# Five small experts of a routed layer: from exact parts in float32r to plain float32 in column strips

## The chip, the core and the metric

The kernel runs on one core of a Trainium2 chip, the other cores idle. The metric is the device time of one execution in microseconds; the time before is the median of three runs. A core has a matrix engine (PE, and PEld for its weight loads), three more engines that compute (DVE, ACT, POOL), SP, which issues most transfers here, and 16 DMA engines between the chip's memory (HBM) and the core's own (SBUF). PE writes its products to PSUM, eight banks of 128 rows by 512 float32 columns.

## The reference, cut to what matters

A network of four layers on 256 tokens of 1024 features, in float32 throughout. The change touches only the last sublayer, a mixture of eight experts, two of them for each token:

```
def moe_swiglu(h, w_router, b_router, w_gate, w_up, w_down):
    logits = (h @ w_router).astype(F32) + b_router.astype(F32)
    top_logits, top_idx = lax.top_k(logits, TOP_K)       # TOP_K = 2 of 8
    ...
    # per expert e: (silu(h @ w_gate[e]) * (h @ w_up[e])) @ w_down[e], times the token's gate
```

Each expert has three matrices of 1024 x 3584 (down: 3584 x 1024). For the inputs of `setup_inputs()` the reference sends 146, 114, 95, 61, 35, 30, 24 and 7 tokens to the eight experts, in falling order: 512 places in all.

## The kernel before

The kernel runs the layers one after the other and streams every weight once, in units of 1 MB ([128, 2048] float32, names `raw`). For products PE takes operands in float32r, a form with fewer bits that a full-width product goes through once. To keep float32 accuracy, `w` (lines 215 to 234) splits each unit in two exact parts: ACT casts 1024 columns at a time to float32r (`hi`, line 229), DVE subtracts (`lo`, line 231). `mm3` (lines 242 to 246) then multiplies three times: hi by hi, lo by hi, hi by lo. A `raw` buffer is free again when its unit is split. In the expert layer there are six: four of the pool `wp` and two of the pool `moew` (lines 221 and 222).

`moe` (from line 1801) orders the experts by their counts: rank 0 has the most tokens. `CAPS` gives the slots of each rank. A one-hot matrix of tokens by slots gathers the slots' features (`gather`, `gather_slim`) and adds the results back to the tokens (`scatter`). An expert's hidden columns come in 7 steps of 512, each of six units: two of gate, two of up, two of down. There are three shapes of work:

- `Narrow` (ranks 1 to 3, 128 slots): slots are the stationary operand, weights move, 512 columns at a time, three products each (`mm3`).
- `Slim` (ranks 4 to 7, 64 slots): both parts of a slot's features are two rows of one product, so that hi and lo of the weights are enough (two products, line 1963); a product with `ii` adds the two rows again (line 1976).
- `wide` (rank 0, 256 slots): the weights are stationary, the slots move, 256 at a time, three products. It is a generator: 21 steps of two units, and two scatters. `turn` calls one step after every third turn of the Slim items, three turns an item (lines 2070 to 2077).

The main loop (lines 2079 to 2102) walks through the items of the ranks 4, 1, 5, 2, 6, 3, 7 and keeps one item ahead: gate of this item, `prep` of the last (transposes), up of this, down of the last. A scheduler places instructions within this order; SP issues the units in the order in which `w` was called, each when its buffer is free. Tokens beyond an expert's slots are handled by code behind a branch (line 2105) that these counts don't enter.

Of the kernel before, what the change touches and what calls it, by code (L numbers as in the profile page):

```python
# [56 lines left out]
def constants():  # L57
# [23 lines left out]
    c["c_ii"] = (t[:, None] % 64 == np.arange(64)[None]).astype(f)  # L81
# [100 lines left out]
# ---------------------------------------------------------------- the program  # L182
class Net:
# [31 lines left out]
    def w(self, src, n=2048):  # L215
        """a weight unit: its raw tile and, in pieces of 1024 columns, its two exact parts;
        the result gives the parts of a range of columns"""
# [3 lines left out]
        self.turn = (self.turn + 1) % 6 if self.more else 0  # L221
        pool, bufs = (self.wp, 4) if not self.more or 0 < self.turn < 5 else (self.more, 2)
# [37 lines left out]
    def rows(self, factors=False):  # L260
        """for products of rows not normed: self.eps, eps for the norms that follow; the factors of the rows' own norm"""
# [9 lines left out]
    def split(self, ps, hi, lo, scale=None):  # L271
        """hi and lo, the exact parts of ps (times the column scale)"""
# [7 lines left out]
    def rms(self, xs, eps=1e-6, pool=None):  # L280
        """x * rstd, token-major"""
# [10 lines left out]
    def norm_t(self, xs, gname, i, perm=False, out=None, xn=None):  # L292
        """feature-major parts of rms_norm(x) * g, its rows normed already; perm: token 8c + 2q + h at column 128h + 32q + c"""
# [23 lines left out]
    def proj_a(self, xt, src, kt=8, mt=2, halves=False):  # L317
        """one unit of columns: feature-major, [128, mt, 256]"""
# [41 lines left out]
    def proj_d(self, xt, src, order=None, end=False):  # L360
        """[256, 1024] = x @ w, token-major, four banks"""
# [80 lines left out]
    # ---- first block  # L442
# [10 lines left out]
    def t5_bias(self, ph):  # L453
        """bias[q, h, c] of the distance 128 + q - c, -1e30 below zero"""
# [52 lines left out]
            # columns: [s0 t0 | s0 t1 | s1 t1]  # L507
# [10 lines left out]
    def out_steps(self, o, src, n=4, done=None):  # L518
        """steps of o @ w, a unit at a time"""
# [81 lines left out]
        # k_idx | w_idx  # L601
# [14 lines left out]
        # norms of c_q and c_kv  # L616
# [21 lines left out]
        # indexer: k_idx feature-major twice over, q_idx feature-major  # L638
# [26 lines left out]
        # a key of the future gets -1e30 exactly, then the 64 largest of each row are marked  # L665
# [14 lines left out]
        # queries, keys and values  # L680
# [27 lines left out]
    def small_a(self, w, xt, n, put):  # L708
        """x of 256 features times w [256, n], feature-major; put(m, psum of two blocks, 2)"""
# [1673 lines left out]
```

## Time and profile before

| | us |
|---|---|
| median of 3 runs | 2505.92 (2504.39 to 2511.6) |
| the profiled execution, its span | 2511.8 |
| first unit of an expert issued at | 1446.49 |
| PE busy, whole span | 2381.2 (95%) |
| DVE busy, whole span | 1850.4 (74%) |
| ACT busy, whole span | 1503.8 (60%) |
| mean rate of the DMA over the span | 236 GB/s |

The span is the time from the first to the last instruction of the program in the profiled execution, the table's second row. A busy PE isn't a PE at its peak: the spacing of the starts in the timeline tells what one product takes, its duration also holds the latency. The expert layer, from 1446 to the end, has 336 units and reads 352.3 MB, three fifths of what the kernel reads in all.

### The profile page before, as it was taken

To read this page: it belongs to the slowest core of one execution; us is meant where nothing else is said; L and a number is where in the kernel's file an instruction comes from. 1 tells how busy PE (TensorE), PEld (TensorE's weight loads), DVE (VectorE), ACT (ScalarE), POOL (GpSimd) and SP (SyncE) were. 2 spreads that over 40 slices of the span, in tenths; PEclk is the share of its full clock that TensorE was granted. 3 is DMA by queue.
4 is the path that set the end of the run, shared out by engine and by line. 5 is a ranking of instruction groups with operands and counts; after the bars stand their busy time and mean duration, and the time that the engine had idled before them with its cause. 6 is when DMAs were issued, how large, how long until landed. Compare 5 with 4: busy or idle time off the path is not lost.

```text
span 2511.8 us, 37371 instructions
## 1 busy us (share of the span) xinstructions
PE 2381.2 (95%) x14223; PEld 2025.2 (81%) x14223; DVE 1850.4 (74%) x2606; ACT 1503.8 (60%) x2256; POOL 169.7 (7%) x153
## 2 busy tenths in 40 slices
PE   8999999989987999999989979999999999999997
PEld 7789888879876787999878868777888778877785
DVE  5566567896787275555667498888888888898888
ACT  5655456634453266444556477777676677676776
POOL 0000003033602000000121000000000000000000
PEclk9999999999998899999999989999999999999999
DMA  7436553555623453555424098889888988889886
GB/s 280 159 137 233 186 188 118 196 179 194 251 93 104 123 216 116 185 186 188 183 101 155 26 361 342 321 341 362 331 323 328 349 340 342 333 311 347 344 323 249
DMA packets 100472, 593.06 MB, mean 236 GB/s; under 512 B 12275, under 2 KB 25748, under 8 KB 32316
## 3 DMA queue, kind: packets, MB, share of 16 engines
q1 hardware_dynamic: 86816, 562.72, 59.9%
q10 hardware_dynamic: 11452, 17.38, 1.9%
q0 software_dynamic: 2016, 10.49, 1.2%
q8 instruction: 114, 1.87, 0.3%
q14 instruction: 74, 0.61, 0.1%
HBM read 571.41 MB, written 19.14 MB: 235 GB/s over the span
## 4 chain that ended last, share of the span: by engine, by line
PE 51%; DVE 6%; ACT 3%; issue 2%; POOL 1%; DMA 0%; ACTq 0%; DVEq 0%; POOLq 0%
PE acc L245 7%; PE acc L244 7%; PE acc L246 7%; PE pt L1963 6%; PE pt L245 6%; PE pt L244 6%; PE pt L246 6%; DVE lo L231 4%; PE acc L1990 3%; ACT hi L229 2%; PE pt L1976 1%; PE pt L920 1%; POOL rstd_r L257 1%; PE pt L1937 0%; DVE x L1896 0%
## 5 line engine op out<-in xcount | busy, mean ns | idle before, releaser
L231 DVE TENSOR_TENSOR lo<-raw,hi 128x1024 fp32r<-128x1024 f32 x1042 | 1251.4, 1242 | 311.9 <-ACT hi L229 310.8
L229 ACT CAST hi<-raw 128x1024 fp32r<-128x1024 f32 x1042 | 1046.9, 1051 | 465.5 <-PE pt L245 161.3
L244 PE MATMUL pt<-xh,hi 128*128 128x256 f32 (+1 forms) x1112 | 314.9, 283 | 2.6 <-DVE xl L278 2.0
L245 PE MATMUL pt<-xl,hi 128*128 128x256 f32 (+1 forms) x1112 | 312.5, 281 | 0.2 <-DVE xl L278 0.2
L246 PE MATMUL pt<-xh,lo 128*128 128x256 f32 (+1 forms) x1112 | 312.3, 281 | 0.0
L244 PEld LDWEIGHTS pt<-xh,hi 128*128 128x128 f32 (+1 forms) x1112 | 210.3, 189 | 8.3 <-issue 2.5
L245 PEld LDWEIGHTS pt<-xl,hi 128*128 128x128 f32 (+1 forms) x1112 | 210.0, 189 | 2.8 <-DVE xl L278 0.6
L246 PEld LDWEIGHTS pt<-xh,lo 128*128 128x128 f32 (+1 forms) x1112 | 210.2, 189 | 0.0
L244 PE MATMUL pt<-hi,xh 128*128 128x256 f32 x512 | 146.5, 286 | 1.4 <-DVE ol L278 1.4
L245 PE MATMUL pt<-lo,xh 128*128 128x256 f32 x512 | 144.4, 282 | 0.0
L246 PE MATMUL pt<-hi,xl 128*128 128x256 f32 x512 | 144.1, 282 | 0.0
L246 PE MATMUL acc<-hi,hlo 128*128 128x512 f32 x344 | 137.3, 400 | 6.3 <-DVE hlo L276 6.3
L244 PE MATMUL acc<-hi,hhi 128*128 128x512 f32 x344 | 137.7, 400 | 3.5 <-ACT hhi L275 3.5
L245 PE MATMUL acc<-lo,hhi 128*128 128x512 f32 x344 | 136.9, 398 | 0.0
L245 PE MATMUL pt<-lo,xgh 128*128 128x512 f32 x336 | 135.9, 405 | 1.0
L244 PE MATMUL pt<-hi,xgh 128*128 128x512 f32 x336 | 133.9, 399 | 2.1 <-DVE x L1896 2.1
L246 PE MATMUL pt<-hi,xgl 128*128 128x512 f32 x336 | 132.8, 395 | 0.0
L245 PE MATMUL acc<-x0l,hi 128*128 128x256 f32 x448 | 124.6, 279 | 0.0
L244 PE MATMUL acc<-x0h,hi 128*128 128x256 f32 x448 | 124.4, 279 | 0.0
L246 PE MATMUL acc<-x0h,lo 128*128 128x256 f32 x448 | 123.9, 280 | 0.0
L244 PEld LDWEIGHTS pt<-hi,xh 128*128 128x128 f32 x512 | 98.8, 193 | 3.3 <-DVE ol L278 2.2
L245 PEld LDWEIGHTS pt<-lo,xh 128*128 128x128 f32 x512 | 98.7, 193 | 0.9 <-DVE lo L231 0.3
(723 smaller groups left out, 4841.3 us busy)
## 6 DMA issues: line engine op xcount, KB each, us to landing
raw<-in_moe_gate SPq DMA_DIRECT2D x112, 1024.0 KB, 6.1
raw<-in_moe_up SPq DMA_DIRECT2D x112, 1024.0 KB, 6.5
raw<-in_moe_down SPq DMA_DIRECT2D x112, 1024.0 KB, 6.8
raw<-in_mlp_up SPq DMA_DIRECT2D x32, 1024.0 KB, 4.8
raw<-in_mlp_dn SPq DMA_DIRECT2D x32, 1024.0 KB, 4.8
raw<-in_ff_g SPq DMA_DIRECT2D x11, 1024.0 KB, 4.8
raw<-in_ff_u SPq DMA_DIRECT2D x11, 1024.0 KB, 4.8
raw<-in_ff_d SPq DMA_DIRECT2D x11, 1024.0 KB, 4.8
```

Of the source, the lines that this page charges most:

```text
L229: nc.scalar.copy(hi[:, :c], raw[:, o:o + c])
L231: nc.vector.tensor_tensor(lo[:, :c], raw[:, o:o + c], hi[:, :c].bitcast(F32), op=OP.subtract)
L244: mm(out, l[0], r[0], start=first, stop=False)
L245: mm(out, l[0], r[1], start=False, stop=False)
L246: mm(out, l[1], r[0], start=False, stop=last)
L257: nc.gpsimd.tensor_tensor(r, v, self.mhalf[:, :width], op=OP.pow)
L920: nc.tensor.matmul(po[:, d * 256:d * 256 + 256], v[:, m, d * 128:d * 128 + 128], PT[:, m * 256:m * 256 + 256], start=m == 0, stop=m == 1)
L1963: mm(p, l, q, start=u + k + i == 0, stop=u * 4 + k + i == 8)
L1976: mm(p[:, o:o + 64], me.z[i][:, j * 128:j * 128 + 128], ii, start=True, stop=True)
L1990: mm(me.acc[c], me.hT[:, 2 * u + j].rearrange("p a c -> p (a c)"), q, start=f + u + j + i == 0, stop=f == 6 and u + j + i == 3)
```

## The change

Ranks 3 to 7 get 64, 64, 32, 32 and 32 slots (before: rank 3 had 128 and the Narrow form, ranks 4 to 7 had 64 and the Slim form). Their weights are not split (`whole=True`): PE takes them from `raw` as plain float32, and the gathered features (`xc`) too, in one tile of 256 columns for all five. A product with 64 (32) slots fills 64 (32) of the array's 128 columns; two (four) such products, each with its own quarter or half of the hidden columns, are issued in turn and write their own rows of one PSUM bank (class `Few`, `strip`). `prep` transposes two (one) blocks, `down` does the same with the output columns in one PSUM bank, and `scatter_few` adds strip by strip. The one-hot rows for it are made again at each expert's sixth item (`few_rows`). The order of the ranks is 3, 1, 4, 2, 5, 6, 7, and a step of `wide` follows every fourth turn in ranks 3 and 4, every third in ranks 5 to 7.

```diff
-CAPS = (256, 128, 128, 128, 64, 64, 64, 64)
+MORE = 2
+CAPS = (256, 128, 128, 64, 64, 32, 32, 32)
...
-    def w(self, src, n=2048):
+    def w(self, src, n=2048, whole=False):
...
         nc.sync.dma_start(raw[:, :n], src)
+        if whole:
+            return lambda o, c: raw[:, o:o + c]
...
+            xg = ph.tile([128, 8, 256], F32, name="xc")
+            for k2 in range(4):
+                p = self.pt()
+                for j in range(2):
+                    for i, src in enumerate((hh, hl)):
                         for t in range(2):
+                            mm(p[:, j * 256:j * 256 + 256], src[:, t, (2 * k2 + j) * 128:(2 * k2 + j + 1) * 128], OH[:, t], start=i + t == 0, stop=i + t == 2)
+                (nc.scalar.copy if k2 % 2 else nc.vector.tensor_copy)(xg[:, 2 * k2:2 * k2 + 2], p.rearrange("p (j c) -> p j c", j=2))
...
+        def scatter_few(acc, OT, r, then=None):
+            n = CAPS[r]
+            G, w = 128 // n, 8 * n
+            y = ph.tile([128, 512], F32, name="yf", bufs=2)
+            nc.scalar.copy(y[:, 0:w], acc[0][:, 0:w])
+            for t in range(2):
+                ps = [self.pt() for _ in range(G)]
+                for g, p in enumerate(ps):
+                    mm(p[:, 0:w], OT[g * n:g * n + n, t * 128:t * 128 + 128], y[g * n:g * n + n, 0:w], start=True, stop=True)
+                for g, p in enumerate(ps):
+                    o = xs[t][:, g * w:g * w + w]
+                    stt(o, p[:, 0:w], gater[:, t, r:r + 1], o, op0=OP.mult, op1=OP.add)
...
-        class Slim:
...
+        class Few:
+            def __init__(me, r, f, xg, acc):
+                me.r, me.f, me.xg, me.acc = r, f, xg, acc
+                me.n = CAPS[r]
+                me.G = 128 // me.n
+                me.w = 4 * me.n
+            def load(me, n):
+                return [unit(n, me.r, 2 * me.f + u, True) for u in range(2)]
+            def strip(me, g):
+                return slice(g * me.n, g * me.n + me.n)
             def col(me, ws):
+                p, x = self.pt(), me.xg()
                 for u, w in enumerate(ws):
                     for k in range(4):
-                        l = x[:, 4 * u + k, me.e].rearrange("p a c -> p (a c)")
-                        for i, q in enumerate(w(k * 512, 512)):
-                            mm(p, l, q, start=u + k + i == 0, stop=u * 4 + k + i == 8)
+                        for g in range(me.G):
+                            mm(p[me.strip(g), 0:me.w], x[:, 4 * u + k, few[me.r]:few[me.r + 1]], w(k * 512 + g * me.w, me.w), start=u + k == 0, stop=u + k == 4)
                 return p
             def fin(me):
+                me.z = ph.tile([128, 512], F32, name="s", bufs=2)
+                nc.scalar.activation(me.z[:, 0:me.w], me.p[0][:, 0:me.w], AF.Silu)
+                tt(me.z[:, 0:me.w], me.z[:, 0:me.w], me.p[1][:, 0:me.w], op=OP.mult)
             def prep(me):
                 p = self.pt()
+                for b in range(me.w // 128):
+                    nc.tensor.transpose(p[:, b * 128:b * 128 + 128], me.z[:, b * 128:b * 128 + 128], self.ident)
+                me.hT = ph.tile([128, 256], F32, name="hTf", bufs=2)
+                nc.scalar.copy(me.hT[:, 0:me.w], p[:, 0:me.w])
             def down(me, ws):
+                nb, c = me.w // 128, 2 * me.w
+                for j in range(4):
+                    g, b = divmod(j, nb)
+                    l = me.hT[:, b * 128 + g * me.n:b * 128 + g * me.n + me.n]
+                    for o in range(me.G):
+                        mm(me.acc[0][me.strip(o), 0:c], l, ws[j // 2](j % 2 * 1024 + o * c, c), start=me.f + j == 0, stop=me.f == 6 and j == 3)
...
-        for r in (4, 1, 5, 2, 6, 3, 7):
+        for r in (3, 1, 4, 2, 5, 6, 7):
...
-            if it and it.r > 3 and "0" in got:
+            if it and it.r > 2 and "0" in got:
                 turns += 1
-                if turns == 3:
+                if turns >= (4 if it.r < 5 else 3):
```

The last item of the layer on PE, before: part of up (`xcl` is the gathered slots), then down from the split parts, and the scatter.

```order
12099 L1963 MATMUL pt<-lo,xcl 128x512
12100 L1990 MATMUL acc<-hi,hTh 128x512 x2
12101 L1990 MATMUL acc<-lo,hTh 128x512 x2
12102 L1990 MATMUL acc<-hi,hTh 128x512 x2
12103 L1976 MATMUL pt<-ii,s 128x64 x2
12104 L1990 MATMUL acc<-lo,hTh 128x512 x2
12105 L1976 MATMUL pt<-ii,s 128x64 x2
```

The same place on PE now: gate, a transpose, up, a transpose, both items' down, the scatter.

```order
10514 L1982 MATMUL pt<-raw,xc 32x128 x16
10515 L1993 MATMUL pt<-ident,s 128x128
10516 L1982 MATMUL pt<-raw,xc 32x128 x48
10517 L1993 MATMUL pt<-ident,s 128x128
10518 L2003 MATMUL acc<-raw,hTf 32x256 x32
10519 L1894 MATMUL pt<-yf,OTf 128x256 x8
```

PE's moving operand is the landed unit itself (`raw`), in pieces of 128 or 256 columns for strips of 32, where before it was a part made of it by ACT or DVE.

ACT at the end of the layer, before: casts of units (`hi`) between the copies and activations of the items.

```order
1184 L1969 COPY s<-pt 128x512
1185 L229 CAST hi<-raw 128x1024 x4
1186 L1969 COPY s<-pt 128x512
1187 L229 CAST hi<-raw 128x1024 x2
1188 L1978 ACTIVATE sz<-pt 128x256
1189 L229 CAST hi<-raw 128x1024
1190 L275 CAST hTh<-sz 128x4x64
1191 L229 CAST hi<-raw 128x1024 x3
1192 L275 CAST hi<-acc 128x512 x2
```

ACT there now: one activation and one copy an item, and a copy of the sum.

```order
995 L1987 ACTIVATE s<-pt 128x128
996 L1995 COPY hTf<-pt 128x128
997 L1987 ACTIVATE s<-pt 128x128
998 L1995 COPY hTf<-pt 128x128
999 L1890 COPY yf<-acc 128x256
```

No cast of a unit stands in this stretch any more; the ones that remain in the layer belong to `wide` and `Narrow`.

## Rows read from the trace of the kernel before

**Rows 1.** The page's slices: busy tenths of 40 equal parts of the span.

```profile
PE   8999999989987999999989979999999999999997
DMA  7436553555623453555424098889888988889886
```

**Rows 2.** Windows: us, busy PE, PEld, DVE, ACT, POOL, clock, DMA share, GB/s.

```profile
1446.50:1460.00 13.50, 4.25 (x19) 4.14 (x20) 12.89 (x46) 8.05 (x14) 0.00 (x0) 0.50 0.89 334
1460.00:1510.00 50.00, 48.45 (x263) 39.55 (x263) 49.73 (x66) 42.24 (x55) 0.00 (x0) 0.99 0.97 388
1446.50:2491.00 1044.50, 1015.20 (x5244) 831.71 (x5245) 904.80 (x947) 751.15 (x887) 0.00 (x0) 0.99 0.88 338
1682.20:1735.60 53.40, 53.15 (x231) 41.46 (x230) 45.30 (x43) 37.71 (x42) 0.00 (x0) 1.00 0.93 355
...
1472.00:1492.00 20.00, 19.17 (x102) 15.18 (x101) 19.99 (x25) 18.33 (x24) 0.00 (x0) 1.00 1.01 423
```

**Rows 3.** Groups from 1400 us on, one: count, busy us, mean ns, idle before.

```profile
L231 DVE TENSOR_TENSOR lo<-raw,hi 128x1024 fp32r<-128x1024 f32 x676 | 787.1, 1222 | 71.1 <-ACT hi L229 70.9
```

**Rows 4.** Timeline of PE, Narrow and wide products: start us, duration us.

```profile
1639.94 0.39 PE L245 MATMUL pt<-lo,xgh 128*128 128x512 f32 x1
1640.17 0.40 PE L246 MATMUL pt<-hi,xgl 128*128 128x512 f32 x1
...
2365.09 0.28 PE L244 MATMUL acc<-x0h,hi 128*128 128x256 f32 x1
2365.21 0.28 PE L245 MATMUL acc<-x0l,hi 128*128 128x256 f32 x1
```

**Rows 5.** Timeline of SP's queue: the first unit's issue, and gates of Narrow items.

```profile
1446.49 0.37 SPq L224 DMA_DIRECT2D raw<-in_moe_gate  x1
...
1700.18 4.91 SPq L224 DMA_DIRECT2D raw<-in_moe_gate  x2
...
1717.89 4.91 SPq L224 DMA_DIRECT2D raw<-in_moe_gate  x2
```

**Rows 6.** The chain that ended last, its longest pieces between 1500 and 1600: Slim.

```profile
1518.24 4.14 PE acc L1990 x16
...
1537.62 1.73 PE pt L1976 x16
1539.35 3.80 PE pt L1963 x16
```

**Rows 7.** Timeline of PE: plain float32, full array and one strip of 32.

```profile
1425.44 1.90 PE L920 MATMUL pt<-PT,v 128*128 128x256 f32 x8
...
843.05 0.38 PE L1749 MATMUL pt<-raw,Xp 128*32 128x128 f32 x2
843.27 0.38 PE L1748 MATMUL pt<-raw,Us 128*32 128x128 f32 x2
```

**Rows 8.** Two strips of 64 in turn: timeline, and groups of 844.23 to 845.31.

```profile
844.24 0.27 PE L1434 MATMUL pt<-U,btt 128*64 128x64 f32 x1
...
845.11 0.28 PE L1434 MATMUL pt<-U,btt 128*64 128x64 f32 x2
845.32 0.41 PE L1748 MATMUL pt<-raw,Us 128*32 128x128 f32 x2
...
L1434 PE MATMUL pt<-U,btt 128*64 128x64 f32 x16 | 1.2, 225 | 0.0
L1433 PE MATMUL pt<-vt,ktt 128*64 128x64 f32 x14 | 1.0, 225 | 0.0
```

**Rows 9.** Timeline of SP's queue at the end: last units, puts of the output.

```profile
2479.85 4.56 SPq L224 DMA_DIRECT2D raw<-in_moe_down  x2
2503.01 3.21 SPq L2066 DMA_DIRECT2D y<-x  x4
```

**Rows 10.** Windows around a fall of PE's granted clock.

```profile
800.00:809.00 9.00, 7.74 (x50) 5.43 (x48) 8.86 (x10) 4.16 (x14) 5.39 (x4) 0.99 0.28 102
809.00:815.00 6.00, 5.05 (x20) 3.58 (x18) 1.03 (x1) 2.40 (x5) 0.00 (x0) 0.50 0.26 80
```

More of the change, by code (lines that the diff above doesn't have):

```diff
@@ L1813, in moe @@
         iota = self.loaded(ph, [128, 256], "iota", a["c_iota"])
-        ii = self.loaded(ph, [128, 64], "ii", a["c_ii"])
         ids = {}
+        few = {3: 0}
+        for r in range(3, 8):
+            few[r + 1] = few[r] + CAPS[r]
         def onehot(o, r, t, base, n):
@@ L1877, in scatter @@
-        def scatter(y, OT, s, r, cs=(0, 1), then=None):
-            if then:
-                parts = [self.wp.tile([128, 1024], F32R, name=n, bufs=6) for n in ("hi", "lo")]
-                parts = [[z[:, c * 512:c * 512 + 512] for z in parts] for c in range(2)]
-                for c in cs:
-                    self.split(y[c], *parts[c])
-            for c in cs:
-                if then:
-                    yh, yl = parts[c]
-                else:
-                    yh, yl = (ph.tile([128, 512], F32R, name=n) for n in ("yh", "yl"))
-                    self.split(y[c], yh, yl)
+                for r in range(3, 8):
+                    onehot(OH[:, t, few[r]:few[r + 1]], r, t, 0, CAPS[r])
@@ new lines, in gather_few, with few_rows @@
+            return xg
+        def few_rows(r):
+            n = CAPS[r]
+            OH = ph.tile([128, 2, 128 // n, n], F32, name="OHf", bufs=1)
+            for t in range(2):
+                ts(OH[:, t], iota[:, 0:n].unsqueeze(1).to_broadcast([128, 128 // n, n]), posr[:, t, r:r + 1], selr[:, t, r:r + 1], op0=OP.is_equal, op1=OP.mult)
+            p = self.pt()
+            for t in range(2):
+                nc.tensor.transpose(p[:, t * 128:t * 128 + 128], OH[:, t].rearrange("p a c -> p (a c)"), self.ident)
+            OT = ph.tile([128, 256], F32, name="OTf", bufs=2)
+            nc.vector.tensor_copy(OT, p[:, 0:256])
+            return OT
@@ new lines, in scatter_few @@
+        def scatter_few(acc, OT, r, then=None):
+            n = CAPS[r]
+            G, w = 128 // n, 8 * n
+            y = ph.tile([128, 512], F32, name="yf", bufs=2)
+            nc.scalar.copy(y[:, 0:w], acc[0][:, 0:w])
+            for t in range(2):
+                ps = [self.pt() for _ in range(G)]
[4 more added lines that the diff above has]
+                    stt(o, p[:, 0:w], gater[:, t, r:r + 1], o, op0=OP.mult, op1=OP.add)
+                    if then and (g + 1) * w % 512 == 0:
+                        then(t, ((g + 1) * w - 1) // 512)
@@ L1890, in scatter @@
+        def scatter(y, OT, s, r):
+            for c in range(2):
+                yh, yl = (ph.tile([128, 512], F32R, name=n) for n in ("yh", "yl"))
+                self.split(y[c], yh, yl)
                 for t in range(2):
@@ L2039, in moe @@
             "a": lambda: gather([(1, 0, 128), (2, 0, 128)]),
-            "b": lambda: gather([(3, 0, 128), (3, 0, 128)]),
-            "c": lambda: gather_slim((4, 5, 6, 7)),
+            "c": gather_few,
         }
@@ L2049, in moe @@
         self.more = es.enter_context(tc.tile_pool(name="moew", bufs=2))
-        items, before, after = [], {}, {}
-        gathers = {(4, 2): "a", (4, 3): "0", (6, 5): "b"}
-        for r in (4, 1, 5, 2, 6, 3, 7):
+        items, before, after, rows = [], {}, {}, {}
+        gathers = {(3, 2): "a", (3, 3): "0"}
+        for r in (3, 1, 4, 2, 5, 6, 7):
             for f in range(7):
@@ L2055, in moe @@
                     before[len(items)] = lambda n=gathers[r, f]: get(n)
-                if r < 4:
-                    n, s = ("a", r - 1) if r < 3 else ("b", 0)
-                    items.append(Narrow(r, f, lambda n=n: got[n][0], s, acc))
-                else:
-                    z, e = divmod(r - 4, 2)
-                    items.append(Slim(r, f, lambda z=z: got["c"][0][z], e, acc))
-            if r < 4:
-                after[len(items) - 1] = lambda n=n, s=s, r=r: scatter(acc, got[n][1], s, r)
+                if r < 3:
+                    items.append(Narrow(r, f, lambda: got["a"][0], r - 1, acc))
+                else:
+                    if f == 5:
+                        before[len(items)] = lambda r=r: rows.update({r: few_rows(r)})
+                    items.append(Few(r, f, lambda: got["c"], acc))
+            if r < 3:
+                after[len(items) - 1] = lambda r=r: scatter(acc, got["a"][1], r - 1, r)
             else:
-                after[len(items) - 1] = lambda z=z, e=e, r=r: scatter(acc, got["c"][1][z], e, r, (0, 1), put if r == 7 else None)
+                after[len(items) - 1] = lambda r=r: scatter_few(acc, rows[r], r, put if r == 7 else None)
         put = lambda t, c: nc.sync.dma_start(out[t, :, c * 512:c * 512 + 512], xs[t][:, c * 512:c * 512 + 512])
@@ L2105, in moe @@
         with tc.If(over > 0):
-            for r in (1, 2, 4, 5, 6):
+            for r in range(1, 8):
                 n = nc.values_load(ints[0:1, 1, r:r + 1], min_val=0, max_val=256)
```

61 lines of the change are left out of this document (7 added, 54 removed).

## Prediction

> **What bounds the kernel now.** I read four views in this order. First the slices of the page: in the last seventeen of the forty, which are the expert layer, PE stands at 9 and DMA at 8 or 9 in every slice but the very last, where the earlier slices show DMA at 0 to 7 [rows 1]. So two resources are near their limit there, and no stretch before the layer is touched by the change. Second the windows of that layer: from the first expert weight to a few us behind the last one's issue, 1044.5 us, PE is busy for 1015.2, DVE for 904.8, ACT for 751.2, and the stream runs at 338 GB/s [rows 2]. PE is the bound. The windows next to it say how much faster the stream can go when nothing holds it: 388 GB/s over 50 us and 423 over 20 us, both at a DMA share near 1 [rows 2]. Third the groups of instructions: 676 subtractions of 1.22 us, 0.79 ms of DVE, end the splits of the weights in two exact parts [rows 3], after as many casts on ACT; two of each a unit. Fourth the timeline, for what PE pays a step.
>
> All eight experts are read whole: 8 x 42 = 336 units of 1.0486 MB, 352.3 MB. The change doesn't lower that. At 388 GB/s a unit takes 2.70 us and the 336 take 908 us, against 1044.5 now. The gain can't pass some 137 us unless the stream goes faster than it has for 50 us; the question is how near it comes.
>
> **The change, part by part.**
>
> PE price of an item before (six units, 512 hidden columns of one expert). A 512-column product starts every 0.233 us [rows 4]. Narrow: 72 of them and four transposes; two gate issues of neighbouring items lie 1700.18 and 1717.89 apart, 17.7 us [rows 5]. Slim: 16 products for each weight, 3.80 us for gate, as much for up, 4.14 for down, and 1.73 for the 16 passes that add its halves, 13.5 us [rows 6]. A step of the widest expert: 96 products of 256 columns at 0.118 [rows 4], 11.3 us for two units. Check: 28 x 13.5 + 21 x 17.7 + 21 x 11.3 = 987, and 28 are left of the 1015 for four gathers and nine scatters.
>
> PE price after. A plain float32 product is recorded as two passes: four products of line 920 give eight passes of 256 columns in 1.90 us; less the 0.38 of a single one's latency, the seven starts lie 0.217 apart [rows 7]. On a strip of 32 a pass of 128 moving columns starts every 0.11 us (two from 843.05 to 843.27) [rows 7]. So a pass costs 0.85 ns a column, and a float32 product of 512 columns 0.87 us in its two passes, nearly four of the 0.233 above. All depends on whether strips run side by side. Lines 1433 and 1434 show it for two strips of 64: 30 passes of 64 columns, which would be 0.054 us each one after the other and 1.63 together, start between 844.24 and 845.17, one every 31 ns [rows 8]. Four strips of 32 in turn are not in this trace; I bound them by two at a time (twice the price below) and four at a time, and take four.
> With 64 slots an item is 8 x 2 x 0.217 = 3.5 us for gate, the same for up, 4 x 4 x 0.217 = 3.5 for down (512 columns), two transposes: 10.6. With 32 slots it is 8 x 2 x 0.109 = 1.7, 1.7, 4 x 2 x 0.217 = 1.7, one transpose: 5.3 (two strips at a time 10.5; at 31 ns a pass, the pace of rows 8, 5.7).
>
> The time by stretches, in the order that the loop now has. `turn` calls a step of the widest expert after every 4 turns of the two 64-slot experts and every 3 of the 32-slot ones: 3 steps in the expert of rank 3, 5 in rank 4, 7 in rank 5, 6 and the first scatter in rank 6, the other in rank 7. A stretch takes the longer of its PE work and its units at 2.70:
> rank 3: 48 units 130; PE 108 and 12 of gathers.
> rank 1: 42 units 113; PE 7 x 17.7 = 124.
> rank 4: 52 units 140; PE 74 + 57 = 131.
> rank 2: as rank 1, 124.
> rank 5: 56 units 151; PE 37 + 79 = 116.
> rank 6: 54 units 146; PE 37 + 68 + 2 = 107.
> rank 7: 42 units 113; PE 39.
> Sum 928. Five of seven stretches go from PE to the stream; ranks 1 and 2 stay PE's, at the 355 GB/s of their row [rows 2]. Split work falls from 336 units to 126, so DVE and ACT are off the path. The raw buffers decide whether the stream is kept fed: six, each free when its unit is split or, now, when PE has used it. During an 11.3 us step 4 units can land, and its own two are free early, so six issues are possible; I see no hole there.
>
> Edits with one answer: the gather of the small experts writes one part where it wrote two (8 copies for 16), the gather of rank 3 ("b") goes, about 4 us of PE (32 products at 0.118) that the stretches above no longer contain; the one-hot rows are made again at item 5 of each expert, two transposes under the stream. More code stands behind the branch for overflow; it isn't run, since the reference routes 146, 114, 95, 61, 35, 30, 24 and 7 tokens to its experts, which the new 256, 128, 128, 64, 64, 32, 32, 32 slots hold.
>
> Beside the 928: the first weight is issued at 1446.5 [rows 5], unchanged. The fill: 334 GB/s in the first 13.5 us [rows 2], 2 us, and perhaps 2 more until the first product: 4. The scatters of ranks 1 and 2 at PE's expense: 4. Switching the array between strips and whole: the rows where line 1434 gives way to 1748 show 0.21 us between starts for a pass of 64 columns, so 0.15 at most is lost [rows 8]; six switches an item and 35 items are 32 us of PE, of which the spare of ranks 3 and 5 to 7 hides all, that of rank 4 (9 us for 6) most. With the holes that a stream so close to its bound has, I put 8 (0 to 40). The end: now 27.4 us pass from the last unit's issue (2484.4) to 2511.8, with its landing, its split, products, another split, sums and puts; the last of the four puts is issued at 2506.2, 5.6 before the end [rows 9]. After, nothing is split: from the last landing, products 0.9, a copy and the products of the scatter 1.5, eight sums of half the width in some 3.3 (estimated from DVE's 1.22 for 1024 columns), 1.2 to the last put's issue and the 5.6: 12.5.
> 1446.5 + 928 + 4 + 4 + 8 + 12.5 = 2403. That is against the profiled execution's span of 2511.8, which is 5.9 above the median of the runs, a factor 0.9977: 2397.
>
> Two rules of the Trainium skill speak against this. In the window of 50 us the stream ran at 388 GB/s [rows 2]. The page "DMA: Bandwidth & Descriptors", section "Where 436 GB/s comes from", says that for loads from HBM the memory side binds, at about 358 GB/s a core; by it the floor would be an estimated 984 us and the gain about half. The row is above it, so I keep 388 and make the other a rival. The page "TensorEngine Tiling (Array Packing)", section "Key Properties", says that a change of tiling mode drains the array; rows 8 bound such a change at 0.15 us, which is in the sum.
>
> **The rivals.**
> A. *The stream saturates near the rate of the Narrow stretches.* No row shows 388 for longer than 50 us; the highest over 53 is 355 [rows 2]. Then a unit takes 2.95 us and 336 take 992: 1446.5 + 992 + 4 + 12.5 = 2455, or 2449 against the median. Against it: in the Narrow stretch PE is full (53.15 of 53.4), so PE and not the stream sets 355. The 358 of the Trainium skill's page would act so.
> B. *The stream does better.* At the 423 GB/s of the 20 us window [rows 2] a unit takes 2.48, and the sum of the longer ones is 119 + 124 + 131 + 124 + 139 + 134 + 104 = 875: 2350, or 2344. Against it: that window lies inside the 50 us one.
> C. *The strips run one after the other* (the other side). Then an item of 64 or 32 slots costs 8 x 2 x 0.434 twice and 4 x 8 x 0.217: 20.8 us. PE work is 35 x 20.8 + 21 x 11.3 + 248 + 20 = 1233 and bounds all: 1446.5 + 1233 + 15 = 2695, or 2688. It becomes slower than before once the new items cost more than about 15 us on the average (35 x 15 + 505 = 1030); the forecast's prices give 7.4 on the average, two strips at a time in the 32-slot ones 10.5. Rows 8 speak against it; the strips there come in one order, two passes a product, as here.
> D. *The granted clock falls.* In ranks 5 to 7 PE waits for the stream a quarter to two thirds of the time. At 809 the clock fell to 0.50 after 9 us in which PE had been busy for 7.74, and it stayed there for 6 us in which PE was busy for 5.05 [rows 10]. At half clock ranks 5 and 6 need up to 232 and 214 of PE instead of 151 and 146; rank 7 78, still below 113. But a PE that has become the bound has no gaps, and the clock was 0.99 over the dense layer [rows 2], so I take a third of the 149: 2447.
> E. *Overflow after all* (a count above its slots in the kernel's own sums): 42 units more for one expert, at least 113 us; about 2510, no change.
>
> **How the numbers follow.** The forecast (388 GB/s within 10 either way, strips side by side) has 0.64, A 0.11, B 0.11, D 0.08, C 0.04, E 0.02. The predicted time is 2397. The forecast's own range is 2375 to 2425 (380 to 400 GB/s, holes from 0 to 40). B ends at 2344, A and D at 2447 to 2455, so the range that leaves out no more than 2 in 10 is 2344 to 2455: it holds the forecast and most of A, B and D. About 0.3% (7.5 us) is what a measurement of this kernel can tell from no change: faster 0.94, same 0.02, slower 0.04, the last being C.
>
> **What the profile after would show.** Right: DMA share 0.95 or more and 380 to 400 GB/s in the windows of ranks 3 to 7, PE waiting for DMA there; Narrow items still 17.7 us apart; 252 casts of weights in the layer, not 672 (two a unit); the strips' passes of 32 slots starting about 27 ns apart; the last put 12 us behind the last landing. Wrong: PE full in ranks 5 to 7 with passes 0.1 us apart (C) or at a clock of 0.5 (D); a DMA share near 1 at 355 GB/s (A); a low DMA share with PE also idle, which would be a wait that I haven't seen, most likely for a raw buffer.

## The result, and the profile after

The changed kernel took 2394.42 us (median of 4 runs, 2390.66 to 2394.8), the kernel before in the same session 2508.76 (2504.39 to 2512.14): ratio 0.9541, 95% interval 0.9522 to 0.9561. The forecast was 2397. The profiled execution spans 2392.5 us.

The page's slices of the changed kernel, which answer [rows 1]:

```profile
PE   8999999989998889999998998999999999898865
PEclk9999999999999899999999998999999999998976
DMA  7436552546651255455543409999899999999998
```

The last 16 digits are the layer of experts. DMA, 8 to 9 before, is 9 in all but two of them, while PE, 9 nearly throughout before, is at 8 or less in six: the first, the eleventh and the last four. The windows of the seven stretches, in the loop's order 3, 1, 4, 2, 5, 6, 7 (us, busy PE, PEld, DVE, ACT, POOL, clock, DMA share, GB/s), answer [rows 2]:

```profile
1436.80:1557.50 120.70, 108.30 (x824) 73.95 (x826) 35.96 (x89) 24.01 (x39) 0.00 (x0) 0.95 0.96 386
1557.50:1680.60 123.10, 121.74 (x537) 91.16 (x533) 97.58 (x94) 78.36 (x87) 0.00 (x0) 1.00 0.94 367
1680.60:1829.90 149.30, 144.93 (x976) 101.56 (x976) 49.55 (x56) 40.33 (x55) 0.00 (x0) 0.99 0.90 354
1829.90:1956.30 126.40, 122.67 (x583) 93.50 (x580) 97.77 (x94) 79.25 (x89) 0.00 (x0) 1.00 0.94 363
1956.30:2108.70 152.40, 139.81 (x1636) 116.74 (x1638) 63.60 (x72) 48.00 (x64) 0.00 (x0) 0.96 0.92 371
2108.70:2262.00 153.30, 136.15 (x1633) 112.05 (x1624) 53.19 (x67) 36.61 (x50) 0.00 (x0) 0.92 0.94 380
2262.00:2379.50 117.50, 80.18 (x1291) 49.23 (x1282) 13.38 (x28) 6.80 (x21) 0.00 (x0) 0.76 0.99 411
...
1436.80:2379.40 942.60, 853.77 (x7451) 638.19 (x7451) 411.04 (x500) 313.36 (x404) 0.00 (x0) 0.94 0.94 375
...
2285.00:2360.00 75.00, 49.28 (x815) 31.06 (x819) 5.09 (x14) 2.87 (x11) 0.00 (x0) 0.74 1.01 420
```

Only rank 7's stretch is the stream's alone: 420 GB/s for 75 us, that is 1.0486 MB in 2.50 us. Over the layer (the row from 1436.8 to 2379.4) DVE is busy 411 us and ACT 313, where it was 905 and 751. The groups from 1400 us on, which answer [rows 3] (252 of the 254 casts lie in the layer, as forecast):

```profile
L233 DVE TENSOR_TENSOR lo<-raw,hi 128x1024 fp32r<-128x1024 f32 x254 | 295.9, 1220 | 61.0 <-ACT hi L231 59.9
L231 ACT CAST hi<-raw 128x1024 fp32r<-128x1024 f32 x254 | 248.9, 1048 | 75.2 <-DMA raw<-in_moe_down 27.1 <-DMA raw<-in_moe_up 17.8 <-DMA raw<-in_moe_gate 15.6
```

SP's queue, for [rows 5]; the first pair shows the Narrow items still 17.7 us apart, the second a pause of the issues (start, duration) during a step of the widest expert in rank 5:

```profile
1645.19 4.90 SPq L224 DMA_DIRECT2D raw<-in_moe_gate  x2
...
1662.88 4.91 SPq L224 DMA_DIRECT2D raw<-in_moe_gate  x2
...
2027.32 2.88 SPq L224 DMA_DIRECT2D raw<-in_moe_up  x2
2039.91 2.94 SPq L224 DMA_DIRECT2D raw<-in_moe_down  x4
```

Nothing is issued from 2030.2 to 2039.9. PE's products of the wide step run from 2024.95 to 2038.85 (with a wait of 0.5 us behind the first four); then come the small expert's, and then a wait for the next wide step's unit:

```profile
2038.78 1.93 PE L2003 MATMUL acc<-raw,hTf 128*32 128x256 f32 x32
2040.53 1.93 PE L1982 MATMUL pt<-raw,xc 128*32 128x128 f32 x64
...
2047.04 0.99 PE L246 MATMUL acc<-hi,wTh 128*128 128x512 f32 x2 [2.44 <-ACT hi L231]
```

The unit issued at 2039.91 is that step's; by the trace it landed 6.0 us later. The end, on PE and SP, for [rows 9]:

```profile
2369.62 1.08 PE L1982 MATMUL pt<-raw,xc 128*32 128x128 f32 x32 [0.95 <-DMA raw<-in_moe_up]
...
2379.52 1.93 PE L2003 MATMUL acc<-raw,hTf 128*32 128x256 f32 x16 [0.45 <-DMA raw<-in_moe_down]
...
2384.11 2.91 SPq L2078 DMA_DIRECT2D y<-x  x4
```

32 passes of four strips in 1.08 us: less the first one's 0.27, 26 ns each. From the last landing to the end it is 13.1 us (2379.4 to 2392.5).

Of the 119.3 us between the two profiled spans, 109.6 lie in the layer (1065.3 us from the first unit's issue to the end before, 955.7 after). The other 9.7 lie ahead of it, where the instructions are the same; with this code unchanged, the layers of the experiments began at 1436.1 to 1444.7 us. So nearly all of it is variation; that the one profile of the kernel before lies 1.8 us above all of these is not explained.

### The profile page after: what moved, and what is told of

Same layout as the page of the kernel before. It is cut to its first block, busy times and chain, and to the rows that moved or that the text cites. A ratio compares the mean times of both kernels' runs of the same rounds, so it can differ in the third digit from the quotient of the medians.

```text
span 2392.5 us, 40231 instructions
## 1 busy us (share of the span) xinstructions
PE 2207.2 (92%) x16418; PEld 1821.6 (76%) x16418; DVE 1347.9 (56%) x2153; ACT 1057.7 (44%) x1765; POOL 169.3 (7%) x154
## 4 chain that ended last, share of the span: by engine, by line
PE 47%; DMA 7%; DVE 3%; ACT 2%; issue 1%; POOL 1%; ACTq 0%; DVEq 0%; POOLq 0%
PE acc L248 7%; PE acc L247 7%; PE acc L246 7%; PE pt L1982 5%; PE pt L247 5%; PE pt L246 5%; PE pt L248 5%; DMA raw<-in_moe_gate 3%; PE acc L2003 3%; DMA raw<-in_moe_down 2%; DVE lo L233 2%; ACT hi L231 1%; DMA raw<-in_moe_up 1%; PE pt L922 1%; POOL rstd_r L259 1%
## 5 line engine op out<-in xcount | busy, mean ns | idle before, releaser
L233 DVE TENSOR_TENSOR lo<-raw,hi 128x1024 fp32r<-128x1024 f32 x622 | 762.5, 1254 | 298.0 <-ACT hi L231 296.1
L231 ACT CAST hi<-raw 128x1024 fp32r<-128x1024 f32 x622 | 630.7, 1048 | 438.2 <-PE pt L247 158.7
L1982 PE MATMUL pt<-raw,xc 128*32 128x128 f32 (+1 forms) x3584 | 205.5, 322 | 20.4 <-DMA raw<-in_moe_up 11.8
L1982 PEld LDWEIGHTS pt<-raw,xc 128*32 128x32 f32 (+1 forms) x3584 | 145.4, 125 | 74.6 <-issue 14.3
L1988 DVE TENSOR_TENSOR s<-s,pt 128x128 f32<-128x128 f32 (+1 forms) x35 | 11.9, 341 | 251.8 <-PE pt L1982 251.8
L246 PE MATMUL acc<-x0h,hi 128*128 128x256 f32 x448 | 129.7, 291 | 14.2 <-ACT hi L231 14.2
L2003 PE MATMUL acc<-raw,hTf 128*32 128x256 f32 (+1 forms) x896 | 103.1, 473 | 15.4 <-DMA raw<-in_moe_down 15.4
L246 PEld LDWEIGHTS acc<-x0h,hi 128*128 128x128 f32 x448 | 88.0, 197 | 18.7 <-ACT hi L231 17.5
```

The source lines that it names most:

```text
L231: nc.scalar.copy(hi[:, :c], raw[:, o:o + c])
L233: nc.vector.tensor_tensor(lo[:, :c], raw[:, o:o + c], hi[:, :c].bitcast(F32), op=OP.subtract)
L246: mm(out, l[0], r[0], start=first, stop=False)
L1982: mm(p[me.strip(g), 0:me.w], x[:, 4 * u + k, few[me.r]:few[me.r + 1]], w(k * 512 + g * me.w, me.w), start=u + k == 0, stop=u + k == 4)
L1988: tt(me.z[:, 0:me.w], me.z[:, 0:me.w], me.p[1][:, 0:me.w], op=OP.mult)
L2003: mm(me.acc[0][me.strip(o), 0:c], l, ws[j // 2](j % 2 * 1024 + o * c, c), start=me.f + j == 0, stop=me.f == 6 and j == 3)
```

## The experiments

What each did by stretch is read from the issues in its trace: us from the issue of a rank's first unit to that of the next rank's, for rank 7 to the last unit's (issues run up to six units ahead of what has landed, so rank 7 can be below its floor). The floor is 2.50 us for each unit. The windows of the experiments are cut up to 3.4 us ahead of these issues.

| kernel | time, us | 3 | 1 | 4 | 2 | 5 | 6 | 7 |
|---|---|---|---|---|---|---|---|---|
| floor (units) | | 115 (46) | 105 (42) | 130 (52) | 105 (42) | 140 (56) | 135 (54) | 110 (44) |
| changed, again (e1) | 2391.8 | 121 | 123 | 149 | 126 | 150 | 150 | 104 |
| split kept (e2) | 2475.9 | 133 | 125 | 161 | 128 | 179 | 174 | 111 |
| casts kept (e9) | 2432.0 | 123 | 123 | 154 | 129 | 168 | 168 | 104 |
| two strips (e3) | 2436.6 | 121 | 123 | 152 | 126 | 175 | 169 | 104 |
| strips serial (e4) | 2579.9 | 158 | 125 | 183 | 130 | 204 | 198 | 117 |
| wide at a quarter (e5) | 2345.4 | 111 | 126 | 131 | 123 | 139 | 137 | 107 |
| seven buffers (e6) | 2376.1 | 119 | 122 | 147 | 126 | 145 | 144 | 101 |
| five buffers (e12) | 2446.2 | 126 | 128 | 150 | 132 | 162 | 168 | 108 |
| wide steps spread (e7) | 2400.2 | 121 | 123 | 149 | 126 | 141 | 149 | 122 |

In e7 the floors of ranks 5, 6 and 7 are 130 (52), 130 (52) and 125 (50).

**e1, the yardstick.** No edit.

> The changed kernel once more, unaltered, as the yardstick for the kernels beside it. Expected: 2390 to 2396 us. A second profile also tells whether the time before the first expert unit (1436.8 us in the first profile of it, 1446.5 us in the one of the kernel before) belongs to the change: the theory that it is variation of the stages ahead of the layer, whose instructions are the same, lets it lie anywhere from 1433 to 1447 us; the rival that the change shortened it wants it within 2 us of 1436.8.

2391.83 us, ratio 0.9525 (0.9509 to 0.9541). Its layer began at 1441.9 and took 950.7: the start moves without the change's doing.

**e2, the split kept.** In `w` the early return for whole units moves behind the loop that splits:

```diff
-        if whole:
-            return lambda o, c: raw[:, o:o + c]
         his, los = [], []
 ...
+        if whole:
+            return lambda o, c: raw[:, o:o + c]
```

> Of the units of the five smallest experts the two exact parts are made again (420 casts on ScalarE, 420 subtractions on VectorE), and nobody reads them; TensorE's work stays as it is in the changed kernel. Theory (what counts is the stream of weights; either engine's share only has to lie below it): VectorE gains 420 x 1.16 = 487 us and comes to about 415 + 487 = 900 of some 960 us; per unit it needs 2.33 us beside a stream of 2.5 us, so it fits on average but not where the wide steps and the scatters add to it: 2405 to 2450 us. Rival 1 (the relief of VectorE is the gain): it comes back to the kernel before, 2480 us or more. Rival 2 (the relief does nothing, the fewer TensorE cycles are the gain): 2394 +- 7 us.

2475.93 us, ratio 0.9866 (0.9849 to 0.9882): 84 us come back, 26 more than my theory's upper end, and nearly all in the stretches with wide steps. VectorE is not full there (145.0 us busy in the mean of ranks 5 and 6, of 177). What grew is a wait of PE. What PE waits for in ranks 5 and 6 (us in total, times, longest), of e1 and then of e2:

```profile
PE acc L246 <- ACT hi L231: 21.3, 10, 3.0
PE acc L248 <- DVE lo L233: 5.1, 8, 1.0
PE acc L247 <- DVE lo L233: 2.0, 3, 1.0
```
```profile
PE acc L246 <- ACT hi L229: 38.6, 12, 4.7
PE acc L248 <- DVE lo L231: 13.6, 8, 2.7
PE acc L247 <- DVE lo L231: 10.5, 5, 2.6
```

At the start of a wide step PE waits for the split of that step's units, 63 us in place of 28. The run also prices PE's relief without the split's: from the kernel before (2510.0 us, run beside it) it is worth 34 us only.

**e9, only the casts kept** (as e2, and the loop skips the subtraction for whole units).

```diff
             nc.scalar.copy(hi[:, :c], raw[:, o:o + c])
+            if whole:
+                continue
```

> Of the split of the five smallest experts' units only ScalarE's half is made again (420 casts, read by nobody); VectorE's 420 subtractions stay out. With both halves the time was 2475.9 us, 84 above the changed kernel. A unit then costs ScalarE 2 x 1.05 = 2.10 us and VectorE nothing; with both it costs VectorE 2 x 1.22 to 1.24 = 2.45 us, beside units that come every 2.50. Theory (the price of the kept split is VectorE's own time, 2.45 us of every 2.50, with no room left for what it does for the wide steps): the casts alone fit: 2392 to 2412 us. Rival (a raw buffer that has to wait for any engine that also serves the wide steps in order is held through them, however short the work): half of the 84 or more comes back, 2430 to 2460 us.

2431.98 us, ratio 0.9699 (0.9682 to 0.9716). The rival's number, 40 us for an engine that has time enough, but mostly not by the rival's way: in ranks 5 and 6 the issues wait for a cast 34 times, 1.5 us at most. PE's waits in ranks 5 and 6, and ACT's queue after a wide step:

```profile
PE acc L248 <- ACT hi L229: 38.8, 12, 4.7
```
```profile
2057.78 2.94 ACT L229 CAST hi<-raw 128x1024 fp32r<-128x1024 f32 x3
2060.62 0.27 ACT L1989 ACTIVATE s<-pt 128x128 f32<-128x128 f32 x1
2060.79 0.25 ACT L1997 COPY hTf<-pt 128x128 f32<-128x128 f32 x1
2060.93 9.71 ACT L229 CAST hi<-raw 128x1024 fp32r<-128x1024 f32 x10
```
```profile
2065.82 1.22 PE L248 MATMUL acc<-hi,wTh 128*128 128x512 f32 x2 [3.57 <-ACT hi L229]
```

ACT works its casts off in order, those that nobody reads among them, and PE's next wide step waits for one in that row. (Of these 3.57 us a part is the landing: by the trace the step's unit came at 2063.6, 1.4 us into the wait.) The windows of ranks 5 and 6, e1 first, show the rest:

```profile
1961.20:2112.50 151.30, 138.93 (x1645) 116.45 (x1647) 64.68 (x73) 48.01 (x64) 0.00 (x0) 0.98 0.94 376
2112.50:2262.10 149.60, 131.65 (x1627) 108.19 (x1618) 53.20 (x67) 36.83 (x50) 0.00 (x0) 0.95 0.95 389
```
```profile
1966.00:2133.80 167.80, 148.36 (x1656) 124.12 (x1657) 64.50 (x74) 116.69 (x137) 0.00 (x0) 0.91 0.86 340
2133.80:2302.70 168.90, 145.36 (x1615) 119.87 (x1607) 52.84 (x67) 114.98 (x134) 0.00 (x0) 0.86 0.85 344
```

Of the 36 us that the two stretches lose, 13 are idle time of PE; 23 are busy time, for the same instructions: the granted clock is 0.91 and 0.86, where it was 0.98 and 0.95 (270.6 us of PE at a mean of 0.965 would be 295 at 0.885; measured 293.7). The means come from stretches at two levels: around the wait above the clock is granted at 1.00 before, at 0.50 (1.2 GHz) behind it, and near 1.00 again after that:

```profile
2056.00:2062.00 6.00, 6.00 (x166) 4.83 (x164) 2.56 (x4) 5.37 (x9) 0.00 (x0) 1.00 0.56 199
...
2066.00:2072.00 6.00, 5.96 (x14) 4.17 (x15) 4.43 (x4) 5.46 (x6) 0.00 (x0) 0.50 1.01 421
2072.00:2078.00 6.00, 6.00 (x26) 4.33 (x25) 1.29 (x2) 3.13 (x4) 0.00 (x0) 0.98 1.01 422
```

A wait costs here twice, as itself and in the clock that falls with it.

**e3, two strips of 64 for 32 slots** (the same `n = 64` stands in `few_rows` and `scatter_few`).

```diff
-                me.n = CAPS[r]
+                me.n = 64
-  mm(p[me.strip(g), 0:me.w], x[:, 4 * u + k, few[me.r]:few[me.r + 1]], ...
+  mm(p[me.strip(g), 0:me.w], x[:, 4 * u + k, few[me.r]:few[me.r] + me.n], ...
```

> The three smallest experts are computed in two strips of 64 rows in place of four strips of 32 (32 of the 64 rows hold tokens of other experts and are left out at the scatter); no split, same units, same order. Theory (the stream bounds ranks 5 to 7, TensorE has room there): an item costs TensorE 10.6 us in place of 5.3, 21 items 111 us more busy time, but only where wide steps fill TensorE does it show: rank 7 (42 units, 105 us of stream against 74 us) loses nothing, ranks 5 and 6 up to 10 us each: 2394 to 2415 us. Rival (TensorE still sets the time in ranks 5 to 7): up to all of the 111 us, at least 2440 us.

2436.6 us, ratio 0.9704 (0.9688 to 0.972). The place was right (ranks 5 and 6, nothing in rank 7), the size was not: PE in rank 5 is busy 168.5 of 174.9 us.

```profile
1965.70:2140.60 174.90, 168.47 (x1115) 122.43 (x1115) 64.73 (x74) 49.47 (x65) 0.00 (x0) 0.99 0.86 333
```

The room that I counted on was not there: in the changed kernel PE has 12.6 and 17.1 us a stretch left in ranks 5 and 6 (152.4 - 139.8 and 153.3 - 136.2), not the 35 that seven items more costly by 5 us need.

**e4, strips one after another.** The same instructions, with the loop over strips outermost in `col` and `down`:

```diff
-                for u, w in enumerate(ws):
-                    for k in range(4):
-                        for g in range(me.G):
+                for g in range(me.G):
+                    for u, w in enumerate(ws):
+                        for k in range(4):
```

> The same matmuls of the five smallest experts, but the loop over the strips is the outermost: all steps of one strip before the next, so that neighbouring matmuls go to the same strip. Theory (strips side by side are what brings TensorE under the stream): an item costs about 20.8 us of TensorE, more than the 15 us of its six units; 35 items x 20.8 = 728 us with 237 us of wide steps and 248 us of the two experts between: near 1210 us in the layer in place of 956: 2600 to 2690 us. Rival (leaving out the split is the gain, the strips are not needed): 2394 +- 10 us.

2579.85 us, ratio 1.0276 (1.0255 to 1.0296): slower than the kernel before, and below the 2600 expected at least. A run of 64 passes on PE (start, duration):

```profile
2453.43 5.55 PE L1982 MATMUL pt<-raw,xc 128*32 128x128 f32 x64
```

(5.55 - 0.27) / 63 = 84 ns a pass in the mean, against 26 in turns over the strips: 3.2 times.

**e5, the wide expert at a quarter.** The edit leaves out three quarters of its products; its units are still loaded and split.

```diff
-                    for k in range(4):
+                    for k in range(1):
-                        for u, w in enumerate(ws):
-                            for j in range(2):
+                        for u, w in list(enumerate(ws))[1:]:
+                            for j in range(1):
```

> Of the products of the wide expert (rank 0) three quarters are left out (of each unit only the first 128 rows are multiplied; in the down projection only the second unit's); its units are still loaded and split, all else stays. Measured so far: in the changed kernel TensorE is busy 140.7 of 146.6 us in rank 4's stretch, 133.5 of 147.7 in rank 5's, 132.2 of 148.2 in rank 6's; undisturbed units come every 2.50 us. Theory (in ranks 4 to 6 TensorE, not the transfers, sets most of the pace, because a wide step occupies it for about 13.7 us against 5 us of its two units): without three quarters of it these stretches fall to their units' pace, 52, 56 and 54 units x 2.5 = 130, 140 and 135 us: together 37 us less, and rank 3's some 3 us less: 2350 to 2362 us. Rival (the transfers pause there because packets are slower or buffers are held by the splits, which stay): 2385 us or more.

2345.41 us, ratio 0.9352 (0.9334 to 0.937). Windows of ranks 4, 5 and 6:

```profile
1677.00:1808.20 131.20, 116.09 (x717) 70.46 (x717) 50.91 (x57) 40.04 (x54) 0.00 (x0) 0.96 0.99 398
1931.90:2069.60 137.70, 101.86 (x1237) 74.56 (x1235) 64.49 (x73) 48.37 (x64) 0.00 (x0) 0.85 1.00 404
2069.60:2209.00 139.40, 91.79 (x1249) 63.50 (x1253) 53.16 (x67) 36.77 (x50) 0.00 (x0) 0.79 1.01 420
```

They fall to their floors, with DMA shares of 0.99 to 1.01. The pauses come from TensorE's wide steps, not from the transfers.

**e6 and e12, seven and five buffers.** In e6, with room made by three small tiles; in e12 only `MORE = 1`.

```diff
-MORE = 2
+MORE = 3
-            OT = ph.tile([128, 256], F32, name="OTf", bufs=2)
+            OT = ph.tile([128, 256], F32, name="OTf", bufs=1)
...
```

> Seven raw buffers for the units in place of six (three small tiles get one buffer in place of two to make room). Theory (ranks 1, 2 and 4 wait for TensorE's throughput, which more buffers don't change; in ranks 5 and 6 TensorE is busy 133 of 148 us and the stream needs 140 and 135, so that there the two alternate and a buffer of 2.5 us more decouples them): ranks 5 and 6 lose 2 to 6 us each: 2382 to 2390 us. Rival 1 (buffers hold the stream everywhere): 2365 us or less. Rival 2 (they hold it nowhere, or the single small tiles cost as much): 2392 +- 3 us.

> Five raw buffers in place of six, nothing else changed. In the changed kernel the issue of units pauses during wide steps (at 1993.8 to 1999.8 us of its profile nothing is issued, and the transfers stand still at 1997 to 2001); a seventh buffer took 16 us off. Theory (a wide step holds the buffers longer than what they cover, and each buffer covers 2.5 us of it): a buffer less costs at least the 16 us and at most 2.5 us for each of 23 wide steps and 14 items of ranks 1 and 2, 92 us: 2408 to 2440 us, in the stretches of ranks 3, 5 and 6 above all. Rival (the seventh buffer's gain was an effect of the tiles that were made single for it): 2392 +- 4 us.

2376.12 us, ratio 0.9469 (0.9452 to 0.9486), and 2446.23, 0.9759 (0.9742 to 0.9775). Both moved further than expected: -16 and +54 us. By stretch two bounds part: rank 4 gains 2 us from a seventh buffer and loses 1 with five, so it is TensorE's; ranks 5 and 6 gain 5 and 6 and lose 11 and 18, so there buffers decide. Ranks 5 and 6 together, worked out from windows and waits as above:

| | length | PE busy | PE idle | of it for casts | clock |
|---|---|---|---|---|---|
| seven (e6) | 290.6 | 270.1 | 20.5 | 9.8 | 0.99, 0.96 |
| six (e1) | 300.9 | 270.6 | 30.3 | 21.3 | 0.98, 0.95 |
| five (e12) | 333.0 | 285.0 | 48.0 | 30.3 | 0.92, 0.90 |
| six, casts kept (e9) | 336.7 | 293.7 | 43.0 | 38.8 | 0.91, 0.86 |
| six, split kept (e2) | 353.7 | 288.9 | 64.8 | 38.6 | 0.91, 0.87 |

During a wide step PE frees no buffer of the other expert, and the issues pause; so the units of the next wide step land late, and PE in its turn waits for their casts. A buffer more lets them be issued sooner. The landings in the traces agree: in ranks 5 and 6 the pauses between them, beyond 2.50 us a unit and counted from 0.5 us on, come to 18 us with seven buffers, 35 with six (the first profile of the changed kernel; 28 in e1) and 62 with five.

The pause at 1993.8 to 1999.8 that the expectation of e12 names is not one of a wide step: PE then works off the last products of rank 2, a Narrow expert, and its scatter. That at 2030.2 to 2039.9 is.

**e7, a wide step every fourth turn throughout.**

```diff
-                if turns >= (4 if it.r < 5 else 3):
+                if turns >= 4:
```

> A wide step after every fourth turn throughout (before: every fourth in ranks 3 and 4, every third in ranks 5 to 7), so that some six wide steps move from ranks 5 and 6 into rank 7, where TensorE is busy 79 of 116 us. Theory (a stretch takes the larger of its units' 2.5 us each and of its TensorE time, and something between where they are close): ranks 5 and 6 with 5.25 steps each need 52.5 units x 2.5 = 131 us against TensorE 37 + 5.25 x 13.7 = 109 us, 16 us each less than now; rank 7 takes 10 to 12 units more, 25 to 30 us: 2383 to 2390 us. Rival (the wide steps cost the same wherever they stand): 2392 +- 3 us.

2400.23 us, ratio 0.9576 (0.9555 to 0.9596). My theory fell, and the rival's 2392 +- 3 missed too. Ranks 5 to 7 took together 7 us more than in e1. The windows of ranks 5 and 6:

```profile
1957.00:2098.10 141.10, 117.19 (x1409) 94.68 (x1408) 54.02 (x62) 40.68 (x55) 0.00 (x0) 0.92 0.93 372
2098.10:2246.70 148.60, 123.83 (x1599) 103.36 (x1602) 42.95 (x56) 29.37 (x43) 0.00 (x0) 0.89 0.95 388
```

With TensorE busy only 117 and 124 us they still lie 11 and 19 above their floors of 130: a wide step's pause goes with it even where TensorE has a sixth of the time to spare. Over ranks 5 to 7 PE waits 30.4 us for casts in place of e1's 21.3; why the order makes it wait longer stays open.

**e8, interleaved.** The loop over items, cut to its core (the sums of ranks 4 and 5 stand in the wide expert's bank, which has no steps then):

```diff
-        for r in (3, 1, 4, 2, 5, 6, 7):
-            for f in range(7):
+        seq = [(3, f) for f in range(7)]
+        for n, m in ((1, 4), (2, 5)):
+            seq += [(r, f) for f in range(7) for r in (n, m)]
+        seq += [(r, f) for r in (6, 7) for f in range(7)]
...
-                if turns >= (4 if it.r < 5 else 3):
+                if turns >= (4 if it.r == 3 else 2):
```

> The order of the items changed: an item of the TensorE-heavy ranks 1 and 2 (17.7 us for six units' 15 us) is followed each time by one of a smaller expert (rank 4's after rank 1's, rank 5's after rank 2's; their sums stand in the wide expert's bank meanwhile), and the wide steps run beside ranks 3, 6 and 7 (every fourth turn in rank 3, every second in 6 and 7). All arithmetic and all units stay. Theory (the layer's 336 units x 2.50 us = 840 us are the floor, what lies above it, 943 - 840 = 103 us, is TensorE outrunning its units in ranks 1, 2, 4 and partly 5 and 6): pairs take max(17.7 + 10.6, 30) and max(17.7 + 5.3, 30) = 30 us, so all stretches come near the floor but for the wide ones, 2 us above it per step: 2310 to 2340 us. Rival 1 (the pauses belong to the transfers): 2392 +- 5 us. Rival 2 (the wide steps crowded into ranks 6 and 7 give the gain back: 14 turns x 10 us hold 20 steps of 13.7 us, TensorE 346 us in a stretch of 311): 2345 to 2375 us.

2358.92 us, ratio 0.9398 (0.9375 to 0.9421). Windows of the two pairs, and of ranks 6 and 7 together:

```profile
1565.10:1781.60 216.50, 210.12 (x1128) 140.23 (x1126) 114.85 (x115) 94.56 (x111) 0.00 (x0) 1.00 1.00 410
1781.60:1993.30 211.70, 186.30 (x1623) 136.22 (x1620) 117.28 (x118) 95.61 (x115) 0.00 (x0) 0.94 1.01 414
1993.30:2345.00 351.70, 323.99 (x3906) 273.91 (x3908) 141.18 (x173) 99.35 (x139) 0.00 (x0) 0.98 0.92 373
```

The pairs run at the stream's pace (84 units in 216.5 and 211.7 us, a floor of 210): TensorE at 97% busy costs only 6 us there, where the items alternate. Ranks 6 and 7, crowded with wide steps, give some back: the time lies above the theory's 2340 and in rival 2's range.

**e10 and e11, interleaved with seven buffers** (e8 and e6 together). The line that differs in e11:

```diff
-                if turns >= (4 if it.r == 3 else 2):
+                if turns >= (3 if it.r == 3 else 2):
```

> Interleaved order (2358.9 us) with seven raw buffers (which took 16 to 17 us off the order of the changed kernel, all of it in stretches with wide steps and in rank 3). Theory (a wide step holds the buffers for longer than six units take to land; in the paired stretches, which run at 2.52 and 2.58 us a unit, a buffer more changes nothing): only ranks 3, 6 and 7 gain, and there TensorE is busy 177 of 186 us in the last stretch: 5 to 12 us: 2347 to 2354 us. Rival (the gains add up): 2342 us or less.

> As the run beside it (interleaved, seven raw buffers), with a wide step after every third turn in rank 3 in place of every fourth, so that one step moves from ranks 6 and 7, where TensorE is the limit, to rank 3's stretch, where it is busy 108 of 120 us. Theory: some 13 us less of TensorE in the last stretches, 5 us of units and at most 13 of TensorE more in rank 3's: 0 to 6 us below the run beside it. Rival (a wide step costs its hole wherever it stands): the same within 3 us.

2352.29 us, ratio 0.9385 (0.9366 to 0.9404), the fastest, and 2353.37 (0.9391, 0.9373 to 0.9408), no difference. The gains don't add up: where the items alternate, the seventh buffer has little left to cover (the pairs take 216 and 210 us in e10, 216 and 211 in e8; rank 3 gains 3 us, ranks 6 and 7 together 1.5).

## Why the prediction was right, and where it was not

*What bound the kernel before.* The forecast took PE's 1015 busy us of 1044 for the bound. Neither half of the change does it alone: strips with the split kept (e2) give 2475.9 us, no split with the strips one after another (e4) 2579.9, both 2391.8. So the split bound the kernel before nearly as closely as PE.

*The stream.* The sum from the first issue to the last landing was 944 us; it is 942.6. That is two errors that cancel, and luck: rival B, which had the unit right and added up in the same way, came to 2344, 50 us short. A unit of the undisturbed stream takes 2.50 us, not 2.70: 336 x 0.20 = 67 us less. And what lies above the units' own time is 942.6 - 840 = 103 us, not 944 - 907 = 37: 66 more. The step that failed is the one on the raw buffers: "six issues are possible; I see no hole there". The six issues are made, but then all six buffers hold units of the other expert that wait for TensorE as well, and the stream stops; e5, e6 and e12 show it. What the sentence left out is the time from an issue to its landing: the units issued at the ends of two wide steps, at 2017.6 and 2039.9, landed 6.3 and 6.0 us later. A step of 11 us and 6 us more are 17, and six buffers cover 15: an estimated 2 us lost a step, some 26 for the 13 steps of ranks 5 and 6, which lie 31 above their floors. Rank 4, put at 140 as the stream's, is TensorE's at 149: it is busy there for 144.9 us, 14 more than the 131 of the sum, and where these lie was not taken apart. Ranks 5 and 6 are at 152 and 153, with floors of 140 and 135 (151 and 146 by the forecast's unit); rank 7, with nothing to stop it, runs at 2.50 a unit.

Rank 7's 420 GB/s refutes rival A's 355, and with it the 358 that the forecast quoted beside it, for this core alone; B's rate was right where nothing interrupts it. The Trainium skill has the rate in "HBM Reference", section "Specifications (TRN2)": a core that streams alone gets about 425 GB/s, more than its share of 358. The 420 of rank 7 agrees.

*The start and the factor.* Two more errors cancel in most part. The layer began 9.7 us earlier than the forecast's 1446.5, so the span came out at 2392.5 and not 2403; and the factor 0.9977 took some 6 us off where the median now lies 1.9 above the profiled span.

*Ranks 1 and 2.* 123 and 126 us for 124, the items 17.7 apart: right.

*The split.* That DVE and ACT leave the path is right: e2 and e9 give its price, 84 us for both halves and 40 for the casts. But it is not enough that an engine's busy time lies below the stream: e9's ScalarE had room, and cost 40 us, because the casts that PE waits for stand in one queue with all others.

*The strips.* 26 ns a pass for the forecast 27: right. Rival C, brought about in e4 by the order of issue, costs less than its 2688 mainly because a pass then takes 84 ns, not the 109 that C took (0.217 for two). Four strips rather than two (e3) are worth 45 us, though the 32-slot items themselves have time enough: it is time that the wide steps need.

*The end.* 13.1 us for 12.5: right.

*The clock (rival D).* It fell, to a mean of 0.76 in rank 7, where it cost nothing (420 GB/s beside it), and to 0.92 in rank 6. Its mechanism is real: in e9 and e12 PE is busy 23 and 14 us longer in ranks 5 and 6 at the lower clock. In the changed kernel it holds an estimated 11 us of these stretches at most (a mean of 0.965 in e1's 301 us); that wasn't tried apart.

*What would show.* DMA shares of 0.95 at 380 to 400 GB/s in ranks 3 to 7 did not come in ranks 4 and 5 (0.90 and 0.92, 354 and 371), and not quite in rank 6 (0.94, 380). That, and not the time, betrayed the failed step; a wait for a raw buffer was the last of the signs of being wrong that the forecast named. Rival E did not occur: the trace has 336 units.

## What to carry to other kernels

A stream through a few buffers is paced by the longest stretch in which nobody frees one, not by any engine's average: compare the buffers' cover (here 6 x 2.5 = 15 us) with the longest step of whoever empties them (11 us) and the time from an issue to its landing (6 us) together, and look whether that step's own next input is behind the pause. Work that nobody waits for should not stand in the queue of an engine that the bound engine waits for, even if it has the time. Where phases with different bounds follow each other, alternate their items: e8 gained 33 us that way. The Trainium skill's "Perfetto Trace Analysis", section "Optimization Strategy", suggests it for kernels whose most contended engine changes; e8 agrees.

## What was unexpected of the hardware

The stream held 410 to 414 GB/s over 210 us in e8's pairs while PE was 88 to 97% busy and DVE and ACT split units, and 420 over 75 us in rank 7: the products slowed the transfers by less than 3%. The order of the same instructions over four column strips changed a pass from 26 to 84 ns.
